# RWKV stage of a two-layer hybrid block: one inverse for both chunks of a step, and the step's preparation written per direction

## The chip, the cores and the metric

One core of one Trainium2 chip runs the whole kernel. The metric is device time in microseconds of one execution; lower is better.

## The reference, cut to what matters

Two layers run over 1024 latent tokens and 256 context tokens with a model width of 1024. Each layer has three branches (gated linear attention, grouped-query attention, RWKV7) and a merge that gates the three. The change is in the RWKV branch, which runs a recurrence forwards and backwards over the tokens, for 8 heads of 64 columns:

```
def step(s, inp):
    r_t, w_t, k_t, v_t, kk_t, a_t = inp
    sa = jnp.einsum('bhvk,bhk->bhv', s, kk_t)
    s = (s * w_t[:, :, None, :] - sa[..., None] * (kk_t * a_t)[:, :, None, :]
         + v_t[..., None] * k_t[:, :, None, :])
    return s, jnp.einsum('bhvk,bhk->bhv', s, r_t)
...
g1, g2, g3 = _split(mg, MERGE_COLS)
m = (jax.nn.sigmoid(g1) * (ya @ w_o_gla) + jax.nn.sigmoid(g2) * (yb @ w_o_att)
     + jax.nn.sigmoid(g3) * (yc @ w_o_rwkv))
```

The kernel does not walk token by token. It takes chunks of 64 tokens, in which the recurrence becomes a set of small matrix products and the inverse of a triangular 64x64 matrix per head and direction.

## The kernel before, in words

The 1280 tokens are 10 tiles of 128. A **step** handles one tile for the forward direction (d = 0) and one for the backward direction (d = 1); it holds two **chunks** of 64 tokens, so a layer has 20 chunks, `q = 2 * step + c`. The RWKV stage of a layer is `rwkv()`, a generator that interleaves five kinds of work, each itself a generator that yields after its matmuls:

- `elem(step)` (L870 to L931), once per step, loads `lt`, `k`, `kk` and `r` for both directions. For each direction it makes the up-projection on TensorE (`ps_t<-lt,wup`), then tanh on ScalarE, a scan, and products on VectorE and GpSimd. They end in `AR` (L910, L912) and `BK` (L920, L924), the two operands of the chunk's products, and `PC`.
- `gram(q)` (L934 to L988), once per chunk, multiplies `BK` with `AR` for each direction (`ps_t<-AR,BK`, 16 instructions), copies one part to `Ms` on ScalarE (L955) and the masked rest to `G` on VectorE (L956), and transposes `BK` into `BKT`. Then it inverts the 16x16 blocks on the diagonal: `Ms` is stored to `nscr` in DRAM (L960), the blocks are loaded as `Lm`, 64 partitions of one 16x16 block each (L962), 15 pairs of VectorE instructions (`mt`, L974, and `acc`, L977) build the inverse in `acc`, which is stored to `tscr` (L978) and, transposed by ScalarE, to `dscr` (L981). `DT` (L983) and `Dg` (L986) load them back in the layout that TensorE wants. `UV` (L945) loads the values.
- `merge(q)` (L991 to L1025) joins the block inverses to the 64x64 inverse `T`. Its first matmuls are `ps_u<-DT,G`; three more rounds follow, each with a copy or an addition into `T` on VectorE (L1021, L1023).
- `chain(q)` (L1027 to L1117) is the recurrence: it uses `T`, `G`, `BKT`, `UV` and the state `S`, and gives `X` (L1050), `UV` (L1061, L1063), the new `S`, and the outputs.
- `finish` (L1119 to L1149) normalises a tile whose two directions are both done.

`spread` runs a set of such generators as threads. Each has a start and an end as shares of the set's time, and the thread that is furthest behind goes next. For each chunk `rwkv()` (L1151 to L1176) makes a set: the chain of `q`, the merge of `q + 1`, `gram(q + 2)` and, for even `q`, `elem` of the next step. So an inverse of chunk `q + 2` starts one whole chain and merge ahead of its own merge.

`weave` (L201) mixes this main thread with fill, the matmuls of `merge_gates` (L1182 to L1210: `ps_mm` and `ps_o` with `wh` and `wl`, 128x512): after each yield of the main thread as much fill is issued as its weight times the ratio allows, and a fill instruction may not be issued before the eighth last yield of the main thread. A scheduler then orders the instructions of each engine; an engine executes its own list in order. The DMAs are issued by SyncE, in order too: one that waits holds up all behind it.

The pools hold three buffers of `G`, `BKT` and `UV`, two of `BK`, four of `AR`, and one each of `Ms`, `Lm`, `acc`, `DT` and `Dg`.

Of the kernel before, what the change touches and what calls it, by code (L numbers as in the profile page):

```python
# [9 lines left out]
F32 = mybir.dt.float32  # L10
F32R = mybir.dt.float32r
AF = mybir.ActivationFunctionType
ALU = mybir.AluOpType
# [16 lines left out]
def consts():  # L30
# [35 lines left out]
    c["ident16"] = np.tile(np.eye(16, dtype=np.float32).reshape(1, 256), (64, 1))  # L66
# [4 lines left out]
def hybrid_kernel(ctx: ExitStack, tc: tile.TileContext, I: dict, C: dict, out: bass.AP):  # L71
# [102 lines left out]
    NSCR = 3  # L174
    nscr, dscr, tscr = [[dt(f"{x}scr{i}", [64, 1040]) for i in range(NSCR)] for x in "ndt"]

# [3 lines left out]
    def full(z):  # L180
        return z.rearrange("(u i) x -> u (i x)", i=4)[:, 0:4096].rearrange("u (s t) -> s u t", t=64)
# [120 lines left out]
    zero = zp.tile([64, 1040], F32, name="zero")  # L302
# [30 lines left out]
    for l in range(DEPTH):  # L333
# [493 lines left out]
        gmask, id16 = rload("gmask", [128, 128]), rload("ident16", [64, 256])  # L827
# [35 lines left out]
        def elem(step):  # L863

            live = need_ctx or step >= 2
            o = {"AR": [], "BK": [], "PC": rp.tile([128, 2, 8], F32, tag="PC", bufs=3, name=nm("PC"))}
            ld = {}
            lt = re_.tile([128, 2, 128], F32, tag="lt", bufs=1, name=nm("lt"))
            for d in range(2):
                c = slice(128 * blk_of(step, d), 128 * blk_of(step, d) + 128)  # L870
                for j in range(2):
                    dma(out=lt[64 * j:64 * j + 64, d], in_=lora[64 * d:64 * d + 64, j, c])
                for x in ("kk", "k", "r"):
                    if x == "r" and not live:
                        continue
                    ld[x, d] = re_.tile([128, 4, 128], F32, tag="ld_" + x, bufs=2, name=nm("ld_" + x))
                    dma(out=ld[x, d], in_=rscr[x][:, c].rearrange("(m p) n -> p m n", p=128))
            for d in range(2):
                t0 = 128 * blk_of(step, d)

                def tk(x):
                    v = ld[x, d]
                    if d:
                        v = v[:, :, ::-1]
                    return v.rearrange("p m (c i) -> p m c i", c=2)

                sc, av = tmp(), tmp()
                pz = [ps("t"), ps("t")]
                for p in range(4):
                    for j in range(2):  # L890
                        hr = slice(64 * j, 64 * j + 64)
                        x = lt[hr, d, :]
                        pe.matmul(pz[j][:, 128 * p:128 * p + 128], wup[d][hr, 128 * p:128 * p + 128], x[:, ::-1] if d else x, start=True, stop=True)
                yield 1.8
                for j, dst, bi, s in ((0, sc, 0, 0.5), (1, av, 2, -0.5)):
                    for p in range(4):
                        act(out=dst[:, p, :], in_=pz[j][:, 128 * p:128 * p + 128], func=AF.Tanh, scale=0.5, bias=prm[:, bi + d, p:p + 1])
                    pool.tensor_scalar(out=dst, in0=dst, scalar1=s, scalar2=s, op0=ALU.mult, op1=ALU.add)
                L = tmp()
                vec.tensor_tensor_scan(out=L.rearrange("p m i -> p (m i)"), data0=smask, data1=sc.rearrange("p m i -> p (m i)"), initial=0.0, op0=ALU.mult, op1=ALU.add)  # L900
                Pt = rp.tile([128, 8, 65], F32, tag="Pt", bufs=1, name=nm("Pt"))
                vec.memset(Pt[:, :, 0:1], 1.0)
                L8 = L.rearrange("p m (c i) -> p (m c) i", c=2)
                act(out=Pt[:, :, 1:65], in_=L8, func=AF.Exp, scale=-DECAY)
                act(out=L8, in_=L8, func=AF.Exp, scale=DECAY)
                vec.tensor_copy(out=o["PC"][:, d, :].unsqueeze(2), in_=Pt[:, :, 64:65])
                Pi = L.rearrange("p m (c i) -> p m c i", c=2)
                AR = rp.tile([128, 4, 2, 2, 64], F32, tag="AR", bufs=4, name=nm("AR"))
                Pv = Pt.rearrange("p (m c) i -> p m c i", c=2)
                vec.tensor_tensor(out=AR[:, :, :, 0, :], in0=Pv[:, :, :, 0:64], in1=tk("kk"), op=ALU.mult)  # L910
                if live:
                    vec.tensor_tensor(out=AR[:, :, :, 1, :], in0=Pv[:, :, :, 1:65], in1=tk("r"), op=ALU.mult)  # L912
                else:
                    vec.memset(AR[:, :, :, 1, :], 0.0)
                BK = rq.tile([128, 4, 2, 2, 64], F32, tag="BK", bufs=2, name=nm("BK"))
                av4 = av.rearrange("p m (c i) -> p m c i", c=2)
                ka = tmp()
                ka4 = ka.rearrange("p m (c i) -> p m c i", c=2)
                pool.tensor_tensor(out=ka4, in0=tk("kk"), in1=av4, op=ALU.mult)  # L919
                vec.tensor_tensor(out=BK[:, :, :, 0, :], in0=ka4, in1=Pi, op=ALU.mult)  # L920
                for p in range(4):
                    pool.tensor_scalar(out=av[:, p, :], in0=av[:, p, :], scalar1=prm[:, 6, p:p + 1], scalar2=prm[:, 7, p:p + 1], op0=ALU.mult, op1=ALU.add)  # L922
                vec.tensor_tensor(out=av4, in0=av4, in1=tk("k"), op=ALU.mult)
                vec.tensor_tensor(out=BK[:, :, :, 1, :], in0=av4, in1=Pi, op=ALU.mult)  # L924
                o["AR"].append(AR)
                o["BK"].append(BK)
                if live:

                    pool.tensor_tensor(out=ka, in0=av[:, :, ::-1] if d else av, in1=ld["r", d], op=ALU.mult)
                    dma(out=wscr[d][:, t0:t0 + 128].rearrange("(m p) n -> p m n", p=128), in_=ka)  # L930
            return o  # L931

        def gram(q, es, step):

            c, e = q % 2, es[step]
            o = dict(e)
            G = rq.tile([128, 2, 2, 4, 128], F32, tag="G", bufs=3, name=nm("G"))
            BKT = rq.tile([128, 2, 4, 128], F32, tag="BKT", bufs=3, name=nm("BKT"))
            UV = rq.tile([128, 2, 4, 2, 64], F32, tag="UV", bufs=3, name=nm("UV"))
            Ms = rq.tile([64, 2, 2, 4, 64], F32, tag="Ms", bufs=1, name=nm("Ms"))  # L940
            o["G"], o["BKT"], o["UV"] = G, BKT, UV
            for d in range(2):
                t0 = 128 * blk_of(step, d)
                v = vtm[d, t0 + 64 * c:t0 + 64 * c + 64, :]
                dma(out=UV[64:128, d].rearrange("p m h i -> p (m h i)"), in_=v)  # L945
            for d in range(2):
                AR, BK = e["AR"][d], e["BK"][d]
                pg = [ps("t"), ps("t")]
                for p in range(4):
                    for h in range(2):  # L950
                        r = slice(64 * h, 64 * h + 64)
                        pe.matmul(pg[h][:, 128 * p:128 * p + 128], BK[r, p, c].rearrange("p a i -> p (a i)"), AR[r, p, c].rearrange("p a i -> p (a i)"), start=True, stop=True)
                yield 2.0
                for h in range(2):
                    act(out=Ms[:, h, d], in_=pg[h][0:64].rearrange("p (u i) -> p u i", u=4)[:, :, 0:64], func=AF.Copy)  # L955
                    vec.tensor_tensor(  # L956
                        out=G[:, h, d], in0=pg[h].rearrange("p (u i) -> p u i", u=4),
                        in1=gmask.unsqueeze(1).to_broadcast([128, 4, 128]), op=ALU.mult)
            ns, ds, ts = nscr[q % NSCR], dscr[q % NSCR], tscr[q % NSCR]
            dma(out=full(ns), in_=Ms.rearrange("p h d m t -> p (h d m) t"))  # L960
            Lm = rq.tile([64, 16, 16], F32, tag="Lm", bufs=1, name=nm("Lm"))
            dma(out=Lm, in_=diag(ns))  # L962
            acc = rq.tile([64, 16, 16], F32, tag="acc", bufs=1, name=nm("acc"))
            vec.tensor_copy(out=acc.rearrange("p a b -> p (a b)"), in_=id16)
            mt = rq.tile([64, 16, 16], F32, tag="mt", bufs=1, name=nm("mt"))
            for d in range(2):
                pt = ps("t")
                for p in range(4):
                    pe.transpose(pt[:, 128 * p:128 * p + 128], e["BK"][d][:, p, c].rearrange("p a i -> p (a i)"), ident)
                yield 0.5  # L970
                act(out=BKT[:, d].rearrange("p m i -> p (m i)"), in_=pt, func=AF.Copy)
# [179 lines left out]
        def rwkv():  # L1151
# [3 lines left out]
            def put(d, key, steps):  # L1155
                d[key] = yield from steps
# [214 lines left out]
```

## Time and profile before

| what | value |
|---|---|
| median of 3 runs | 4006.45 us (4003.45 to 4014.16) |
| the profiled execution | 3994.97 us |
| its span | 3993.2 us |
| TensorE busy | 3737.1 us, 94% |
| weight loads of TensorE busy | 3135.2 us, 79% |
| VectorE busy | 2101.7 us, 53% |
| ScalarE busy | 1649.8 us, 41% |
| GpSimd busy | 934.1 us, 23% |
| mean granted clock of TensorE | 0.958 |
| the RWKV stages in the span | 1022 to 1856 us and 3030 to 3760 us |

PE is TensorE's matmuls, PEld its weight loads, DVE VectorE, ACT ScalarE, POOL GpSimd, SP SyncE. Busy shares are means over all stages. The granted clock is a share of full speed (2.4 GHz). A wait is an engine's idle time, put down to the work whose end released it. Names such as `ps_t<-AR,BK` are output and inputs of an instruction by the names of the program. A line that reads L85 is that of the helper through which all matmuls go, so matmuls are told apart by their tiles.

### The profile page before, as it was taken

How to read it: one execution, taken by the hardware profiler on the slowest of the kernel's cores; microseconds unless marked ns; L12 is line 12 of the kernel's file. 1: busy time of each engine (PE TensorE's matmuls, PEld its weight loads, DVE VectorE, ACT ScalarE, POOL GpSimd, SP SyncE). 2: the span in 40 equal slices, each digit the busy share in tenths (PEclk: the TensorE clock that was granted, in tenths of full speed). 3: DMA queues.
4: the chain of work that ended last, by engine and by line, in shares of the span. 5: the costliest groups of instructions: out<-in, count | busy, mean ns of one | idle time of the engine just before them, and what ended most of it. 6: DMA issues, size and time to landing. Idle time of an engine off the chain costs nothing.

```text
span 3993.2 us, 82346 instructions
## 1 busy us (share of the span) xinstructions
PE 3737.1 (94%) x32356; PEld 3135.2 (79%) x32356; DVE 2101.7 (53%) x4932; ACT 1649.8 (41%) x4135; POOL 934.1 (23%) x1072
## 2 busy tenths in 40 slices
PE   5999999999889898899998999999998898988999
PEld 3699888888777787677877898888886776766787
DVE  3234445456576676654453244455565766665462
ACT  3244435456434444434133344354474334344322
POOL 2133220000232322310333042300002323223042
PEclk7999999999989999999999999999998899889999
DMA  7723225312365667556544132253124556655553
GB/s 228 247 59 89 55 79 169 103 54 84 99 146 124 143 157 187 146 135 193 159 139 132 52 96 70 76 159 116 48 70 108 117 128 143 152 136 134 178 157 113
DMA packets 826613, 497.24 MB, mean 125 GB/s; under 512 B 303152, under 2 KB 760176, under 8 KB 824176
## 3 DMA queue, kind: packets, MB, share of 16 engines
q1 hardware_dynamic: 826224, 491.97, 45.0%
q8 instruction: 254, 4.16, 0.5%
q14 instruction: 135, 1.11, 0.1%
HBM read 340.02 MB, written 151.81 MB: 123 GB/s over the span
## 4 chain that ended last, share of the span: by engine, by line
PE 68%; DMA 11%; DVE 8%; POOL 4%; issue 4%; ACT 3%; SPq 2%; POOLq 0%; DVEq 0%; ACTq 0%
PE ps_mm L85 27%; PE ps_a L85 17%; PE ps_o L85 12%; PE ps_u L85 6%; PE ps_t L90 3%; PE ps_t L85 2%; DMA nscr<-Ms 2%; DMA Lm<-nscr 2%; POOL tmp L922 1%; DVE mt L974 1%; DVE acc L977 1%; DMA wr<-in_w_in_dram 1%; DVE wl L343 1%; DMA tscr<-acc 1%; POOL tmp L919 1%
## 5 line engine op out<-in xcount | busy, mean ns | idle before, releaser
L85 PE MATMUL ps_mm<-h,wh 128*128 128x512 f32 (+1 forms) x2496 | 764.5, 389 | 10.1 <-ACT wh L342 7.7
L85 PEld LDWEIGHTS ps_mm<-h,wh 128*128 128x128 f32 x2496 | 452.5, 196 | 105.2 <-issue 11.7
L343 DVE TENSOR_TENSOR wl<-wr,wh 128x512 fp32r<-128x512 f32 (+1 forms) x464 | 334.5, 743 | 296.7 <-ACT wh L342 292.5
L85 PE MATMUL ps_mm<-h,wl 128*128 128x512 f32 (+1 forms) x1248 | 473.8, 380 | 1.7 <-DVE wl L343 1.7
L342 ACT ACTIVATE wh<-wr 128x512 fp32r<-128x512 f32 (+1 forms) x464 | 271.5, 622 | 420.1 <-PE ps_mm L85 161.4
L85 PE MATMUL ps_mm<-wh,h 128*128 128x256 f32 x2032 | 400.4, 290 | 9.5 <-ACT wh L342 5.9
L85 PEld LDWEIGHTS ps_mm<-wh,h 128*128 128x128 f32 x2032 | 327.7, 194 | 26.0 <-issue 10.7
L85 PE MATMUL ps_a<-h,wh 128*128 128x512 f32 (+1 forms) x1024 | 300.1, 369 | 0.0
L85 PE MATMUL ps_mm<-wl,h 128*128 128x256 f32 x1016 | 293.4, 289 | 0.4 <-DVE wl L343 0.2
L85 PE MATMUL ps_o<-h,wh 128*128 128x512 f32 (+1 forms) x928 | 287.7, 392 | 0.6 <-DVE M L1265 0.6
L85 PEld LDWEIGHTS ps_mm<-h,wl 128*128 128x128 f32 x1248 | 243.6, 195 | 47.8 <-issue 4.0
L974 DVE TENSOR_TENSOR mt<-Lm,acc 64x15 f32<-64x15 f32 (+2 forms) x600 | 129.4, 216 | 163.7 <-DMA Lm<-nscr 146.0
L803 POOL TENSOR_TENSOR y<-y,sg 128x128 f32<-128x128 f32 x64 | 30.2, 472 | 755.1 <-DVE nb L794 369.0
L85 PEld LDWEIGHTS ps_a<-h,wh 128*128 128x128 f32 x1024 | 183.7, 189 | 28.3
L85 PEld LDWEIGHTS ps_mm<-wl,h 128*128 128x128 f32 x1016 | 196.7, 194 | 7.4 <-issue 4.9
L85 PE MATMUL ps_o<-wh,h 128*128 128x256 f32 x976 | 196.7, 289 | 3.5 <-ACT h L286 3.2
L85 PEld LDWEIGHTS ps_o<-h,wh 128*128 128x128 f32 x928 | 167.9, 197 | 34.2 <-issue 2.2
L85 PE MATMUL ps_a<-h,wl 128*128 128x512 f32 (+1 forms) x512 | 188.6, 368 | 0.0
L776 DVE TENSOR_REDUCE mx<-ps_mm 128x1 f32<-128x512 f32 (+1 forms) x200 | 117.9, 594 | 111.1 <-PE ps_mm L85 108.0
L85 PE MATMUL ps_o<-h,wl 128*128 128x512 f32 (+1 forms) x464 | 176.1, 380 | 0.0
L85 PEld LDWEIGHTS ps_o<-wh,h 128*128 128x128 f32 x976 | 158.5, 193 | 10.7 <-issue 5.3
L1006 POOL COPY T<-Dg 128x512 f32<-128x512 f32 x40 | 30.0, 749 | 566.2 <-DMA Dg<-dscr 527.2
(326 smaller groups left out, 8125.2 us busy)
## 6 DMA issues: line engine op xcount, KB each, us to landing
wr<-in_w_in_dram SPq DMA_DIRECT2D x376, 256.0 KB, 3.5
tg<-th SPq DMA_DIRECT2D x96, 256.0 KB, 3.4
th<-tg SPq DMA_DIRECT2D x96, 256.0 KB, 2.9
wm<-in_w_mod_dram SPq DMA_DIRECT2D x16, 1024.0 KB, 7.1
ld_k<-rscr_k SPq DMA_DIRECT2D x40, 256.0 KB, 3.6
ld_kk<-rscr_kk SPq DMA_DIRECT2D x40, 256.0 KB, 3.7
UV<-vtm SPq DMA_DIRECT2D x80, 128.0 KB, 3.2
nscr<-Ms SPq DMA_DIRECT2D x40, 256.0 KB, 3.8
```

The source lines that it names most:

```text
L85: PE.last = nc.tensor.matmul(*a, **k)
L90: PE.last = nc.tensor.transpose(*a, **k)
L342: act(out=hi, in_=src, func=AF.Copy)
L343: vec.tensor_tensor(out=lo, in0=src, in1=hi.bitcast(F32), op=ALU.subtract)
L776: vec.tensor_reduce(out=mx[:, i:i + 1], in_=s[:, :n], axis=AX.X, op=ALU.max, negate=True)
L803: pool.tensor_tensor(out=y[:, hc], in0=y[:, hc], in1=sg[:, hc], op=ALU.mult)
L919: pool.tensor_tensor(out=ka4, in0=tk("kk"), in1=av4, op=ALU.mult)
L922: pool.tensor_scalar(out=av[:, p, :], in0=av[:, p, :], scalar1=prm[:, 6, p:p + 1], scalar2=prm[:, 7, p:p + 1], op0=ALU.mult, op1=ALU.add)
L974: vec.tensor_tensor(out=mt[:, :n, :w], in0=Lm[:, j, j + 1:16].unsqueeze(2).to_broadcast([64, n, w]), in1=acc[:, j:j + 1, :w].to_broadcast( ...
L977: vec.tensor_tensor(out=acc[:, j + 1:16, :w], in0=acc[:, j + 1:16, :w], in1=mt[:, :n, :w], op=ALU.add)
L1006: pool.tensor_copy(out=T.rearrange("p d m t -> p (d m t)"), in_=Dg.rearrange("p d m t -> p (d m t)"))
```

## The change

The diff replaces `gram(q)` and its place in the schedule.

- `prep(os, step)` prepares both chunks of a step: elementwise work of direction 0, products of both chunks for direction 0, elementwise work of direction 1, products of both chunks for direction 1, then one `inverse(step)`. Each chunk's `Ms` goes to its half of a scratch of 128 rows.
- `inverse` loads one `Lm` with 128 partitions (64 blocks of either chunk), runs the 15 pairs of products once, and stores `tscr` and `dscr` once. `DT` and `Dg` are loaded per chunk.
- `elem` has a direction as its argument; `lt` has two buffers of one direction each.
- `G` and `BKT` have four buffers, `Dg` two; `DT` shares two buffers with `Ms`; `acc`, `mt` and `Lm` have 128 partitions; there are two scratches in place of three.
- `UV` is loaded in `merge`.
- `rwkv()` makes a set of threads per step: both chains in turn, the merge of the second chunk (0 to 0.35), `prep` of the next step (0 to 0.6), and the merge of the next step's first chunk (0.75 to 1).
- `dynamic_dma_scratch_size=1024` is given when the program is made. All DMAs of the kernel are on SyncE's queue.

The core of the diff:

```diff
+        def prep(os, step):
+            e = {}
+            yield from elem(step, 0, e)
+            o = [chunk(step, c, e) for c in range(2)]
+            Ms = [None, None]
+            for c in range(2):
+                Ms[c] = rq.tile([64, 2, 2, 4, 64], F32, tag="Ms", bufs=2, name=nm("Ms"))
+                yield from gram(o[c], c, 0, Ms[c])
+            yield from elem(step, 1, e)
+            for c in range(2):
+                yield from gram(o[c], c, 1, Ms[c])
+                dma(out=full(nscr[step % NSCR], c), in_=Ms[c].rearrange("p h d m t -> p (h d m) t"))
+            yield from inverse(step, o)
+            os[2 * step], os[2 * step + 1] = o
...
+        def inverse(step, o):
+            ns, ds, ts = nscr[step % NSCR], dscr[step % NSCR], tscr[step % NSCR]
+            Lm = rq.tile([128, 16, 16], F32, tag="Lm", bufs=1, name=nm("Lm"))
             dma(out=Lm, in_=diag(ns))
+            acc = rq.tile([128, 16, 16], F32, tag="acc", bufs=1, name=nm("acc"))
...
             for j in range(15):
                 n, w = 15 - j, j + 1
                 vec.tensor_tensor(
+                    out=mt[:, :n, :w], in0=Lm[:, j, j + 1:16].unsqueeze(2).to_broadcast([128, n, w]),
+                    in1=acc[:, j:j + 1, :w].to_broadcast([128, n, w]), op=ALU.mult)
                 vec.tensor_tensor(out=acc[:, j + 1:16, :w], in0=acc[:, j + 1:16, :w], in1=mt[:, :n, :w], op=ALU.add)
+                if j % 5 == 4:
+                    yield 0.0
             dma(out=diag(ts), in_=acc)
...
+            for c in range(2):
+                DT = o[c]["DT"] = rq.tile([64, 2, 2, 4, 64], F32, tag="Ms", bufs=2, name=nm("DT"))
+                dma(out=DT.rearrange("p h d m t -> p (h d m) t"), in_=full(ts, c))
...
+            for w in spread([(prep(os, 0), 0.0, 0.7, whole_prep), (merge(os, 0), 0.8, 1.0, whole_merge)]):
                 yield 2.5 * w
-            for q in range(nq):
-                ths = [(chain(q, os.pop(q)), 0.0, 1.0, 8.3 + 6 * 2.0 + 12 * 2.0 if q % 2 else 8.3 + 6 * 2.0)]
-                if q + 1 < nq:
-                    ths.append((merge(os, q + 1), *((0.4, 0.9), (0.65, 1.0))[q % 2], 3.3 + 4 * 2.0))
-                if q + 2 < nq:
-                    ths.append((put(os, q + 2, gram(q + 2, es, (q + 2) // 2)), *((0.55, 0.9), (0.1, 0.5))[q % 2], 5.0 + 6 * 2.0))
-                if q % 2 == 0 and q // 2 + 1 < NTILE and q:
-                    ths.append((put(es, q // 2 + 1, elem(q // 2 + 1)), *(0.0, 0.45), 3.6 + 4 * 2.0))
+            for step in range(NTILE):
+                ths = [(both(step), 0.0, 1.0, whole_chain), (merge(os, 2 * step + 1), 0.0, 0.35, whole_merge)]
+                if step + 1 < NTILE:
+                    ths.append((prep(os, step + 1), 0.0, 0.6, whole_prep))
+                    ths.append((merge(os, 2 * step + 2), 0.75, 1.0, whole_merge))
                 yield from spread(ths)
```

How the order of the instructions changes shows at two places, both around the merge of a step's first chunk in the second layer. On TensorE before, chunk 2's merge (`ps_u<-DT,G`) stands behind the end of the preceding merge and the chain's product with `X` and `T`; `ps_mm` is fill, `ps_t<-lt,wup` the up-projection of the next step:

```order
L90 MATMUL ps_t_33704<-c_ident,BK_33095 128x128 x4
L90 MATMUL ps_t_33716<-c_ident,BK_33157 128x128 x4
L85 MATMUL ps_u_33493<-T_33348,ET_32612 16x16 x16
L85 MATMUL ps_t_33903<-lt_33884,wup_32272 128x128 x4
L85 MATMUL ps_t_33904<-lt_33884,wup_32272 128x128 x4
L85 MATMUL ps_a_33620<-X_33552,T_33348 64x64 x5
L85 MATMUL ps_a_33621<-X_33552,T_33348 64x64 x5
...
L85 MATMUL ps_u_33763<-DT_33545,G_33392 64x48 x16
```

Its inverse was made from products that stand ahead of the whole chain of the chunk before.

On TensorE with the change the same merge stands behind the up-projection and the first products of the step after it (`AR_33484`, `BK_33487`), with three fill matmuls in between:

```order
L85 MATMUL ps_mm_33227<-h_22963,wh_33217 128x512 x2
L85 MATMUL ps_mm_33227<-h_22963,wl_33218 128x512
L85 MATMUL ps_t_33427<-lt_33416,wup_31887 128x128 x4
L85 MATMUL ps_t_33428<-lt_33416,wup_31887 128x128 x4
L85 MATMUL ps_t_33504<-AR_33484,BK_33487 128x128
L85 MATMUL ps_t_33505<-AR_33484,BK_33487 128x128
...
L85 MATMUL ps_mm_33689<-h_22956,wh_33679 128x512 x2
L85 MATMUL ps_mm_33689<-h_22956,wl_33680 128x512
L85 MATMUL ps_u_33287<-DT_33272,G_32848 64x48 x16
```

So the merge has moved from behind a whole chain to right behind the next step's first products. On VectorE with the change, the middle of the 15 pairs of that inverse (`mt_33237`, `acc_33235`) holds the elementwise work of the next step (`AR_33484`, `BK_33487`, which the products above need):

```order
L987 TENSOR_TENSOR acc_33235<-acc_33235,mt_33237 128x11x5
L933 TENSOR_TENSOR AR_33484<-Pt_33479,ld_kk_33419 128x8x64
L935 TENSOR_TENSOR AR_33484<-Pt_33479,ld_r_33423 128x8x64
L984 TENSOR_TENSOR mt_33237<-Lm_33233,acc_33235 128x10x6
L943 TENSOR_TENSOR BK_33487<-tmp_33488,tmp_33477 128x8x64
L925 MEMSET Pt_33773 128x8
L987 TENSOR_TENSOR acc_33235<-acc_33235,mt_33237 128x10x6
L984 TENSOR_TENSOR mt_33237<-Lm_33233,acc_33235 128x9x7
L946 TENSOR_TENSOR tmp_33426<-tmp_33426,ld_k_33421 128x512
L987 TENSOR_TENSOR acc_33235<-acc_33235,mt_33237 128x9x7
L947 TENSOR_TENSOR BK_33487<-tmp_33426,tmp_33477 128x8x64
L984 TENSOR_TENSOR mt_33237<-Lm_33233,acc_33235 128x8x8
```

Before, the products of the inverse that this merge needs (`acc_33474`, the last pairs) stand among the chain's and the merge's copies, with no `AR` or `BK` between them:

```order
L974 TENSOR_TENSOR mt_33476<-Lm_33472,acc_33474 64x3x13
L343 TENSOR_TENSOR wl_33870<-wr_33871,wh_33869 128x512
L977 TENSOR_TENSOR acc_33474<-acc_33474,mt_33476 64x3x13
L343 TENSOR_TENSOR wl_33870<-wr_33875,wh_33869 128x512
L974 TENSOR_TENSOR mt_33476<-Lm_33472,acc_33474 64x2x14
L956 TENSOR_TENSOR G_33597<-ps_t_33659,gmask_32268 128x512
L956 TENSOR_TENSOR G_33597<-ps_t_33660,gmask_32268 128x512
L977 TENSOR_TENSOR acc_33474<-acc_33474,mt_33476 64x2x14
L1023 COPY T_33348<-ps_u_33450 32x8x32
L974 TENSOR_TENSOR mt_33476<-Lm_33472,acc_33474 64x15
L977 TENSOR_TENSOR acc_33474<-acc_33474,mt_33476 64x15
```

The pairs of the inverse and the next step's elementwise work share one stretch of VectorE's list now.

## Rows read from the trace of the kernel before

**Rows 1.** The page, busy time, share and instructions of each engine.

```profile
PE 3737.1 (94%) x32356; PEld 3135.2 (79%) x32356; DVE 2101.7 (53%) x4932; ACT 1649.8 (41%) x4135; POOL 934.1 (23%) x1072
```

**Rows 2.** Table by stage: stretch, length, busy (count) per engine, granted clock, DMA share, GB/s.

```profile
1022.00:1856.00 834.00, 748.33 (x9352) 614.32 (x9352) 521.38 (x1255) 342.29 (x770) 227.02 (x242) 0.93 0.61 148
3030.00:3760.00 730.00, 647.54 (x8368) 511.88 (x8368) 463.47 (x1160) 286.29 (x651) 209.79 (x217) 0.90 0.56 133
```

**Rows 3.** Table by stretch, around a wait of 4 us.

```profile
1390.00:1396.00 6.00, 2.70 (x75) 2.46 (x71) 4.97 (x6) 1.82 (x4) 4.16 (x4) 0.96 1.03 215
1396.00:1404.00 8.00, 7.31 (x121) 6.87 (x123) 7.94 (x15) 3.22 (x10) 4.44 (x5) 0.61 1.03 277
```

**Rows 4.** Waits of TensorE: what released it, us in total, times, longest.

```profile
PE ps_u L85 <- DMA DT<-tscr: 22.2, 11, 4.3
PE ps_t L85 <- DVE BK L924: 20.6, 7, 8.0
PE ps_u L85 <- DVE T L1021: 17.2, 10, 4.0
PE ps_a L85 <- DVE X L1050: 11.6, 6, 3.7
```

**Rows 5.** Groups by line on VectorE: count, busy us, mean ns, idle before.

```profile
L977 DVE TENSOR_TENSOR acc<-acc,mt 64x15 f32<-64x15 f32 (+2 forms) x600 | 130.2, 217 | 17.0
L974 DVE TENSOR_TENSOR mt<-Lm,acc 64x15 f32<-64x15 f32 (+2 forms) x600 | 129.4, 216 | 163.7 <-DMA Lm<-nscr 146.0 <-DMA dscr<-accT 2.2
L1061 DVE COPY UV<-ps_a 64x512 f32<-64x512 f32 x40 | 27.0, 676 | 5.1 <-PE ps_a L85 4.7
L1050 DVE TENSOR_TENSOR X<-ps_a,X 128x512 f32<-128x512 f32 x38 | 26.2, 690 | 7.3 <-PE ps_a L85 6.4
```

**Rows 6.** Timeline of TensorE (start, us): last products of a chunk, and its merge.

```profile
1191.23 1.16 PE L85 MATMUL ps_t<-AR,BK 64*128 64x128 f32 x8
...
1223.09 1.14 PE L85 MATMUL ps_u<-DT,G 64*64 64x48 f32 x32
```

**Rows 7.** Timeline of SyncE's queue, the same inverse.

```profile
1196.33 0.60 SPq L962 DMA_DIRECT2D Lm<-nscr  x1
...
1209.48 0.62 SPq L978 DMA_DIRECT2D tscr<-acc  x1
...
1212.16 0.59 SPq L983 DMA_DIRECT2D DT<-tscr  x1
```

**Rows 8.** Timeline of VectorE, first and last of that inverse's 30 products.

```profile
1198.94 0.18 DVE L974 TENSOR_TENSOR mt<-Lm,acc 64x15 f32<-64x15 f32 x1 [1.14 <-DMA Lm<-nscr]
...
1209.29 0.17 DVE L977 TENSOR_TENSOR acc<-acc,mt 64x15 f32<-64x15 f32 x1
```

**Rows 9.** The page, DMA issues: count, KB each, us to landing.

```profile
DT<-tscr SPq DMA_DIRECT2D x40, 256.0 KB, 4.3
Dg<-dscr SPq DMA_DIRECT2D x80, 128.0 KB, 4.2
```

**Rows 10.** Timeline of TensorE: 16 products, then fill matmuls in threes.

```profile
1355.61 1.16 PE L85 MATMUL ps_t<-AR,BK 64*128 64x128 f32 x16
1356.70 0.73 PE L85 MATMUL ps_mm<-h,wh 128*128 128x512 f32 x2
...
1357.51 0.62 PE L85 MATMUL ps_mm<-h,wh 128*128 128x512 f32 x2
```

**Rows 11.** Timeline, end of an up-projection on TensorE and its BK on VectorE.

```profile
1511.18 0.80 PE L85 MATMUL ps_t<-lt,wup 64*128 64x128 f32 x4
...
1522.55 0.69 DVE L924 TENSOR_TENSOR BK<-tmp,tmp 128x512 f32<-128x512 f32 x1
```

**Rows 12.** Timeline of TensorE, the stage's first up-projection and the products behind it.

```profile
1051.28 1.71 PE L85 MATMUL ps_t<-lt,wup 64*128 64x128 f32 x16
...
1061.84 2.08 PE L85 MATMUL ps_t<-AR,BK 64*128 64x128 f32 x16 [7.96 <-DVE BK L924]
```

**Rows 13.** Loads of the tile Lm, us from issue to landing.

```profile
DMA to landing us min/median/max: 2.5/2.9/5.5
```

More of the change, by code (lines that the diff above doesn't have):

```diff
@@ L172, in hybrid_kernel, with full @@
     yscr, wscr = dt("yscr", [512, NT]), [dt(f"wscr{i}", [512, NT]) for i in range(2)]
-    NSCR = 3
-    nscr, dscr, tscr = [[dt(f"{x}scr{i}", [64, 1040]) for i in range(NSCR)] for x in "ndt"]
+    NSCR = 2
+    nscr, dscr, tscr = [[dt(f"{x}scr{i}", [128, 1040]) for i in range(NSCR)] for x in "ndt"]
     def diag(z):
         return z[:, 0:1024].rearrange("p (s t) -> p s t", t=64)[:, :, 0:16]
-    def full(z):
-        return z.rearrange("(u i) x -> u (i x)", i=4)[:, 0:4096].rearrange("u (s t) -> s u t", t=64)
+    def full(z, c):
+        return z[64 * c:64 * c + 64].rearrange("(u i) x -> u (i x)", i=4)[:, 0:4096].rearrange("u (s t) -> s u t", t=64)
     def xrow(l, t):
@@ L878, in elem @@
[L878 to L888, printed above, removed]
-                for p in range(4):
[L890 to L953, printed above, removed]
-                for h in range(2):
[L955 to L961, printed above, removed]
@@ new lines, in elem @@
+            lt = re_.tile([128, 128], F32, tag="lt", bufs=2, name=nm("lt"))
+            c = slice(128 * blk_of(step, d), 128 * blk_of(step, d) + 128)
+            for j in range(2):
+                dma(out=lt[64 * j:64 * j + 64], in_=lora[64 * d:64 * d + 64, j, c])
+            for x in ("kk", "k", "r"):
+                if x == "r" and not live:
+                    continue
+                ld[x, d] = re_.tile([128, 4, 128], F32, tag="ld_" + x, bufs=2, name=nm("ld_" + x))
+                dma(out=ld[x, d], in_=rscr[x][:, c].rearrange("(m p) n -> p m n", p=128))
@@ new lines, in elem, with tk @@
+            t0 = 128 * blk_of(step, d)
+            def tk(x):
+                v = ld[x, d]
+                if d:
+                    v = v[:, :, ::-1]
+                return v.rearrange("p m (c i) -> p m c i", c=2)
+            sc, av = tmp(), tmp()
+            pz = [ps("t"), ps("t")]
+            for p in range(4):
+                for j in range(2):
+                    hr = slice(64 * j, 64 * j + 64)
+                    x = lt[hr, :]
+                    pe.matmul(pz[j][:, 128 * p:128 * p + 128], wup[d][hr, 128 * p:128 * p + 128], x[:, ::-1] if d else x, start=True, stop=True)
@@ new lines, in elem @@
+            ka = tmp()
+            ka4 = ka.rearrange("p m (c i) -> p m c i", c=2)
+            pool.tensor_tensor(out=ka4, in0=tk("kk"), in1=av4, op=ALU.mult)
+            vec.tensor_tensor(out=BK[:, :, :, 0, :], in0=ka4, in1=Pi, op=ALU.mult)
+            for p in range(4):
+                pool.tensor_scalar(out=av[:, p, :], in0=av[:, p, :], scalar1=prm[:, 6, p:p + 1], scalar2=prm[:, 7, p:p + 1], op0=ALU.mult, op1=ALU.add)
+            vec.tensor_tensor(out=av4, in0=av4, in1=tk("k"), op=ALU.mult)
@@ L966, in gram @@
[L966 to L971, printed above, removed]
+            mt = rq.tile([128, 16, 16], F32, tag="mt", bufs=1, name=nm("mt"))
             for j in range(15):
@@ L993, in merge @@
             G, Dg, DT = o["G"], o["D"], o["DT"]
+            UV = o["UV"] = rq.tile([128, 2, 4, 2, 64], F32, tag="UV", bufs=3, name=nm("UV"))
+            for d in range(2):
+                t0 = 128 * blk_of(q // 2, d) + 64 * (q % 2)
+                dma(out=UV[64:128, d].rearrange("p m h i -> p (m h i)"), in_=vtm[d, t0:t0 + 64, :])
             T = o["T"] = rq.tile([128, 2, 4, 64], F32, tag="T", bufs=3, name=nm("T"))
```

105 lines of the change are left out of this document (67 added, 38 removed).

## The prediction

> **What bounds the kernel now.** I read the page first, for the engines' shares; then the table by stage, for the two stretches that the change touches; then the waits of TensorE, for what ends its idle time there; last the timeline, for how long one inverse takes and how long one elementwise part takes. The page says that TensorE is busy for 94% of the span [rows 1]. The table by stage gives the two RWKV stages, 834 and 730 us long [rows 2]. TensorE is idle in them for 85.7 + 82.5 = 168 us. The granted clock is 0.93 and 0.90 there, so that full speed for the whole stage would save at most 0.07 x 834 + 0.10 x 730 = 131 us. The clock comes from gaps: after a wait of 4 us the chip grants the 1.2 GHz level, and the 8 us around it run at a mean of 0.61, which costs 0.39 x 8 = 3.1 us [rows 3]; 131 / 3.1 makes about 42 such falls. So some 299 us of 1564 can be won, and all else is matmuls that the change leaves as they are. The waits of TensorE say what the idle time consists of: 22.2 us for DT, the inverse on its way back from DRAM, 20.6 for BK, 17.2 for T and 11.6 for X, with many small ones besides [rows 4]. VectorE is busy for 985 of 1564 us [rows 2], so it sets the end only where a chain runs through it.
>
> **The change part by part, VectorE.** The products of the inverses take 129.4 + 130.2 us for 1200 instructions [rows 5]. With 128 partitions 600 are left. A copy of 64 partitions takes 676 ns and an addition of 128 partitions with the same 512 elements each takes 690 [rows 5], so a product keeps its length and VectorE loses 130 us of work. What stood behind those products wins: T, X, G and BK come sooner. Of the 168 us of idle time 146 are left when DT's 22 are taken out; waits for ScalarE, for tables and for products of TensorE itself stay. I let half of the 146 go: **-73**. The ends are 0, if what is late there is late for another reason, and -102 (70%).
>
> **DT's old waits.** The 11 waits of 22.2 us [rows 4] were those of chunks whose inverse came late; their places are new now, and the new ones are counted below: **-22**.
>
> **The new boundary.** What the order shows decides. One inverse in the trace: the last matmul of its chunk's products ends at 1192.4 [rows 6], Lm is issued at 1196.33 [rows 7], the 30 products run from 1198.94 to 1209.46 with other work of VectorE among them [rows 8], the store tscr is issued at 1209.48 and the load DT at 1212.16, 2.7 us later [rows 7], and DT lands 4.3 us after that [rows 9]: 24.1 us in all. Nobody waited, since the merge that needs it began at 1223.09, 30.7 us after the product [rows 6]. With two chunks in one inverse the first merge of a pair has less behind which to hide. I laid the durations of the timeline (1.09 us for 16 of the products and about as much for a group of 32 small matmuls, 0.81 for three fill matmuls; start to start [rows 10]) on TensorE's order of both kernels. Before, the even chunks have 19.5 to 32.1 us of work between their last product and their merge. Now they have 7.5 to 24.8.
>
> For eleven of the twenty pairs it is worse than a short cover: VectorE has the elementwise work of the next pair's first direction inside the 30 products, and TensorE has that direction's up-projection (ps_t<-lt,wup) just ahead of the merge. So the inverse cannot end before the next BK. In the trace the up-projection ends at 1511.98 and BK at 1523.24, 11.3 us later [rows 11]. Add 1 us for the products that stand behind BK (one to four pairs in most of the eleven, 0.22 us each [rows 5]), 2.7 for the store [rows 7], 4.3 for the load [rows 9]: DT lands 19.3 us after the up-projection. The work between it and the merge is, for the eleven, 1.1, 4.6, 3.0, 5.7, 1.1, 1.9, 2.0, 4.6, 3.8, 3.8 and 3.8 us, 35.4 in sum. So 11 x 19.3 - 35.4 = **177 us** of new waits, first for BK (the products of the next pair follow the up-projection with 0 to 3.5 us between) and then for DT. Behind the waiting matmul stand the fill, the later rounds of that merge and the chain of the next pair, so nothing fills the gap. The other nine have the plain 24.1 us against covers of 22.2, 18.1, 16.7, 24.8, 20.9, 21.1, 20.9, 20.0 and 18.4: shortfalls of 1.9, 6.0, 7.4, 0, 3.2, 3.0, 3.2, 4.1 and 5.7, **34.5 us**.
>
> Bounds: once in the trace, at the stage's start, the products follow their up-projection at once; TensorE then begins them 8.9 us after its end, 7.96 of them waiting [rows 12]. The shortest landing of such a load is 2.5 us [rows 13]. A boundary could so cost 8.9 + 1 + 2.7 + 2.5 = 15.1, the eleven 11 x 15.1 - 35.4 = 131, and the other nine, with 22.3, 20. Upwards, the larger Lm (twice the rows, 2.9 us now [rows 13]) could take as long as DT, 4.3, which adds 1.4 to each of the nine. I take nothing for it, since Dg with 128 KB lands in 4.2 and DT with 256 KB in 4.3 [rows 9]. The Trainium skill ("DMA: Bandwidth & Descriptors", section "Anatomy of one DMA — SWDGE (gpsimd) path") gives about 2.0 us plus the bytes at 436 GB/s, for a DMA that GpSimd issues. By it the store would take 2.3 and the load 2.6, an estimate of 2.1 us less for each of twenty boundaries, some 40 us less in the sum; the rows, 2.7 and 4.3 on SyncE's queue, are longer, so this trace does not bear it out and the rows stand.
>
> **Clock.** 42 falls go with 168 us of idle time. With 73 us of the old idle time left, 73/168 of them, 18, stay, and 15 of the new waits are longer than the 4 us of rows 3 (the eleven, and four of the nine): 33 in place of 42, **-28 us** at 3.1 each. The ends are -59 (23 left) and 0.
>
> **What costs nothing.** 60 DMAs fewer on SyncE's queue (Lm, tscr and dscr are issued once for two chunks): it waits for nothing that TensorE lacks other than DT. The UV load now stands in the merge, behind DT and Dg on that queue; its user is the chain after the merge, several rounds later. DT takes the buffers of Ms, so the next pair's copies to Ms wait for the merge that reads DT; the merge stands right behind those products in the order, and the transposes that need the bank come after. The prologue's changed weight moves three fill groups.
>
> **Sum.** On the profiled execution of 3994.97: +177 +34.5 -73 -22 -28 = +88.5, 4083.5. The median of the runs shown, 4006.45, stands 11.5 above that execution, so the time is **4095**. Its own range goes from the low ends of the waits with my gains (+131 +20 -123 = +28, 4035) to my waits with half of the -73 and no gain in the clock (+211.5 -36 -22 = +153, 4160).
>
> **The rivals.** *Faster.* VectorE's relief is the larger term. For it speaks that T, X, G and BK account for much of the idle time [rows 4] and that the products are what stands ahead of them; against it, that the new order leaves TensorE nothing between the up-projection and the products. With the low ends (+131 +20) and the high gains (-102 -22 -59) the sum is -32: 3963, median 3974. It decides where the eleven waits fall below a mean of 8.0 us with my gains ((73 + 22 + 28 - 34.5) / 11), or below 14.8 us with the high gains ((183 - 20) / 11); I have 177 / 11 = 16.1. Chance 0.30. *No change.* The waits only change places: TensorE's matmuls are the same, VectorE is not full, and what is lost at eleven boundaries returns in the rest, 4006. The Trainium skill ("Perfetto Trace Analysis", section "Identifying the Most-Contended Engine") says to improve the most contended engine first; the change relieves the engine with 53% [rows 1] and leaves the one with 94% its work. By that rule the time stays near 4006. Chance 0.10. *Much slower.* The half of the old waits does not go, since BK's path rather than the products made them, the clock gains nothing, and the second direction's products (8 to 12 us behind their up-projection in most pairs, against 11.3) wait a further 1 us each, 20 us: +177 +34.5 -22 +20 = +210, 4216 at the median. Chance 0.10.
>
> **How the numbers follow.** My forecast has 0.50. A measurement of this kernel can tell 0.3%, 12 us, from no change. Faster by more: the first rival, 0.30. Within: the second, 0.10. Slower: forecast and third, 0.60. The range runs from 3950, below the first rival, to 4210, just short of the third's value; what is left out is 0.2 at most. Forecasts of both signs hold most of the chance, which is why it is wide; the likeliest case's own is 4035 to 4160.
>
> **What would show it.** Right: TensorE's waits for DT and BK sum to 200 us or more in place of 43, in gaps of 8 to 17 us, one per pair; VectorE has 300 + 300 products with the same mean of 216 ns; waits for T and X are about halved; the stages are longer by some 40 to 45 us each. Wrong: DT and BK together below 100 us, or the elementwise path from the up-projection to BK well under 9 us, or products of 128 partitions that take longer than 64.

## The result and the profile after

The changed kernel takes **4169.47 us** at the median of 4 runs (4168.85 to 4178.87), against 4007.47 before: a ratio of 1.041, 95% interval 1.039 to 1.043. The forecast was 4095, slower by 2.2%; it is slower by 4.1%. The profiled execution has a span of 4167.0 us, 174 more than before.

The table by stage, the changed kernel's two RWKV stages (columns as in [rows 2]):

```profile
1020.00:1928.00 908.00, 761.66 (x9348) 627.77 (x9347) 468.60 (x945) 339.84 (x760) 223.47 (x242) 0.90 0.57 136
3096.00:3940.00 844.00, 672.26 (x8404) 540.22 (x8405) 418.17 (x853) 286.02 (x645) 190.82 (x218) 0.86 0.51 118
```

The stages grew from 1564 to 1752 us. TensorE's idle time in them went from 168 to 146.3 + 171.7 = 318 us, its busy time from 1396 to 1434 (36 more instructions lie inside my second cut, 4 fewer in the first). VectorE has 98 us less work there (985 to 887 [rows 2]).

The waits of TensorE in the changed kernel (columns as in [rows 4]):

```profile
PE ps_u L85 <- DMA DT<-tscr: 128.2, 20, 9.8
PE ps_t L85 <- DVE BK L947: 127.0, 21, 11.2
PE ps_t L85 <- DVE acc L987: 10.1, 1, 10.1
PE ps_t L85 <- ACT accT L992: 9.8, 1, 9.8
PE ps_u L85 <- DVE T L1036: 4.6, 3, 2.3
```

The two single waits of 10 us stand at `ps_t<-AR,BK` too, so DT and BK make 275 us, against 22.2 + 20.6 = 43 [rows 4]. DT is waited for once per step, 20 times. All else fell from 125 to 43 us; T at its first addition, 17.2 us before [rows 4], has 4.6.

The products, groups by line on VectorE in the changed kernel (count, busy us, mean ns, idle before); half as many, with means of 267 and 251 ns in place of 217 and 216 [rows 5]:

```profile
L987 DVE TENSOR_TENSOR acc<-acc,mt 128x15 f32<-128x15 f32 (+2 forms) x300 | 80.2, 267 | 8.0
L984 DVE TENSOR_TENSOR mt<-Lm,acc 128x15 f32<-128x15 f32 (+2 forms) x300 | 75.3, 251 | 69.1 <-DMA Lm<-nscr 61.7
```

TensorE's products of `BK` and `AR`, before and with the change (columns as in [rows 5]):

```profile
L85 PE MATMUL ps_t<-AR,BK 64*128 64x128 f32 x1280 | 128.0, 306 | 35.6 <-DVE BK L924 20.6 <-ACT Pt L904 9.0 <-DVE G L956 5.4
L85 PE MATMUL ps_t<-AR,BK 64*128 64x128 f32 x1280 | 159.4, 323 | 146.9 <-DVE BK L947 127.0 <-DVE acc L987 10.1 <-ACT accT L992 9.8
```

The same 1280 instructions take 31 us more. A group of 16 (one chunk, one direction) that stands in one stretch takes 1.16 us [rows 10], and in the trace its products start in pairs, some 6 ns apart. Eight that stand alone start one by one and take 1.16 us as well, so a group in two halves costs twice as much:

```profile
1122.22 1.16 PE L85 MATMUL ps_t<-AR,BK 64*128 64x128 f32 x8
...
1126.17 1.16 PE L85 MATMUL ps_t<-AR,BK 64*128 64x128 f32 x8
```

Of the 80 groups in the two stages 56 stood in one stretch before and 38 do now; the halves of 8 that stand alone went from 22 to 80. Why the scheduler parts them isn't shown.

One step boundary in the second layer, timeline of TensorE:

```profile
3428.96 1.16 PE L85 MATMUL ps_t<-lt,wup 64*128 64x128 f32 x16
...
3441.43 2.08 PE L85 MATMUL ps_t<-AR,BK 64*128 64x128 f32 x16 [8.45 <-DVE BK L947]
3452.16 1.95 PE L85 MATMUL ps_u<-DT,G 64*64 64x48 f32 x32 [8.65 <-DMA DT<-tscr]
```

The same boundary on VectorE (end of BK, last product) and on SyncE's queue:

```profile
3440.60 0.69 DVE L947 TENSOR_TENSOR BK<-tmp,tmp 128x512 f32<-128x512 f32 x1
...
3442.92 0.17 DVE L987 TENSOR_TENSOR acc<-acc,mt 128x15 f32<-128x15 f32 x1
```

```profile
3443.13 1.22 SPq L990 DMA_DIRECT2D tscr<-acc  x1
3444.44 0.91 SPq L993 DMA_DIRECT2D dscr<-accT  x1
3445.40 1.80 SPq L901 DMA_DIRECT2D ld_r<-rscr_r  x1
3447.30 1.32 SPq L996 DMA_DIRECT2D DT<-tscr  x2
```

The up-projection ends at 3430.12 and BK at 3441.29, 11.2 us later (11.3 in [rows 11]). The last products end 1.8 us behind BK. The load DT is issued 4.2 us after the store (2.7 in [rows 7]) and has landed by 3452.16, 4.9 us after its issue. So 22.0 us lie between the up-projection and DT, where the prediction had 19.3.

The clock around it (table by stretch):

```profile
3428.00:3436.00 8.00, 4.99 (x59) 3.45 (x57) 7.48 (x21) 2.48 (x9) 4.00 (x5) 0.99 0.65 182
3436.00:3444.00 8.00, 2.08 (x16) 1.81 (x16) 6.93 (x20) 1.89 (x3) 3.06 (x4) 0.50 0.31 91
3444.00:3452.00 8.00, 0.00 (x0) 0.00 (x0) 0.29 (x1) 0.00 (x0) 0.00 (x0) 0.50 0.92 140
3452.00:3460.00 8.00, 7.84 (x75) 6.22 (x76) 2.40 (x4) 1.48 (x5) 1.23 (x2) 0.51 0.53 67
3460.00:3468.00 8.00, 8.00 (x145) 6.57 (x143) 2.00 (x4) 2.96 (x7) 0.00 (x0) 1.00 0.37 100
```

The clock falls to the 1.2 GHz level in the first wait, stays there through the products between the two waits, the second wait and 8 us behind it: 24 us, where a single wait of 4 us left some 6 [rows 3]. Cut to 1 us, the table by stage shows 40 stretches of low clock (mean under 0.75) in the two stages before, 255 us in all, and 31 in the changed kernel, 418 us: fewer falls, each 13.5 us instead of 6.4. But most of what was added is waiting: TensorE is busy in 214 of the 255 us and in 217 of the 418. Its busy time at the full level rose from 1182 to 1217 us.

### The profile page after: what moved, and what is told of

It reads as the page before. It is cut to its first block, busy times and chain, and to the rows that moved or that the text cites. A ratio compares the mean times of both kernels' runs of the same rounds, so it can differ in the third digit from the quotient of the medians.

```text
span 4167.0 us, 81524 instructions
## 1 busy us (share of the span) xinstructions
PE 3766.2 (90%) x32356; PEld 3170.0 (76%) x32356; DVE 2003.2 (48%) x4312; ACT 1645.5 (39%) x4115; POOL 914.8 (22%) x1072
## 4 chain that ended last, share of the span: by engine, by line
PE 46%; DMA 4%; DVE 4%; issue 3%; POOL 2%; ACT 1%; SPq 1%; POOLq 0%; DVEq 0%; ACTq 0%
PE ps_mm L85 18%; PE ps_a L85 10%; PE ps_o L85 8%; PE ps_u L85 5%; PE ps_t L85 2%; PE ps_t L90 2%; DMA DT<-tscr 1%; DVE mt L984 1%; DVE acc L987 1%; DMA tscr<-acc 1%; POOL tmp L945 1%; DMA nscr<-Ms 1%; DMA Lm<-nscr 1%; DMA ys<-yTgla 0%; POOL tmp L942 0%
## 5 line engine op out<-in xcount | busy, mean ns | idle before, releaser
L85 PE MATMUL ps_t<-AR,BK 64*128 64x128 f32 x1280 | 159.4, 323 | 146.9 <-DVE BK L947 127.0
L85 PEld LDWEIGHTS ps_t<-AR,BK 64*128 64x128 f32 x1280 | 134.2, 221 | 171.2 <-issue 143.4
L966 DVE TENSOR_TENSOR G<-ps_t,gmask 128x512 f32<-128x512 f32 x160 | 106.2, 687 | 237.9 <-ACT Ms L965 237.7
L921 POOL TENSOR_SCALAR tmp<-tmp 128x512 f32<-128x512 f32 x80 | 53.7, 672 | 708.9 <-ACT tmp L920 696.6
L85 PE MATMUL ps_u<-DT,G 64*64 64x48 f32 x1280 | 61.4, 259 | 128.2 <-DMA DT<-tscr 128.2
```

The costliest lines, as they stand in the source:

```text
L85: PE.last = nc.tensor.matmul(*a, **k)
L966: vec.tensor_tensor(out=o["G"][:, h, d], in0=pg[h].rearrange("p (u i) -> p u i", u=4), in1=gmask.unsqueeze(1).to_broadcast([128, 4, 128]), ...
```

## The experiments

Each has its ratio to the kernel before from its own comparison. "DT and BK" are the waits counted as above, with the few at the same place that the trace puts down to ScalarE's `Pt`; "other" is the rest of TensorE's idle time in the two stages. In these terms: before 52 and 116, the change 275 and 43. Low clock is counted as above.

**Two inverses in the new order.**

```diff
-            yield from inverse(step, o)
+                yield from inverse1(step, c, o)
```

(within the loop over the chunks; `inverse1` is the old inverse on 64 partitions; the buffers, the place of the `UV` load and the scratch size of the change stay)

> The changed kernel with its inverse made per chunk on 64 partitions again (1200 products, a Lm, tscr and dscr each); the order of elementwise work and products, the threads and the buffers stay. Theory (the new order of the work makes the time, through waits for BK behind the up-projection and for DT at the first merge of a step): the time stays near the changed kernel's 4169, between 4110 and 4190; BK's and DT's waits sum to about 200 to 240 us (275 in the changed kernel, 43 before), and waits for T and X come back in part. Rival (the shared inverse makes the time, since the first chunk waits for the second one's products and the wide products are slower): 4000 to 4060, DT's waits near the 22 of before.

4177.91 us, 1.043 (1.041 to 1.045), beside 1.041 for the change: the intervals overlap. DT and BK 171, other 99, granted clock 0.939. The theory's time held, with smaller waits than it said. The shared inverse isn't the loss; undoing it gains nothing in this order. TensorE's idle time in the stages fell from 318 to 270 us, but its busy time rose from 1434 to 1490: the waits are more and shorter, 47 falls of the clock, and matmuls run at the low level for 336 us instead of 217.

**Elementwise work of both directions first.**

```diff
             yield from elem(step, 0, e)
+            yield from elem(step, 1, e)
...
-            yield from elem(step, 1, e)
```

> The changed kernel with the elementwise work of both directions ahead of the products of both; all else as in the change. Theory (the order): the up-projection now has more work between it and its products, BK's waits fall from 137 to about 60 us, DT's stay near 110 to 130, the falls of the clock become fewer, and the time falls to 4030 to 4080. Rival 1 (the shared inverse): above 4140, since the inverse is unchanged. Rival 2 (waits change places, each us saved at BK is waited for DT): above 4140 with DT's waits at 200 or more.

4111.32 us, 1.027 (1.025 to 1.028). BK's waits by name fell from 127 to 43, DT's rose from 128 to 138. Between theory and rivals: about 58 us come from the placement of the elementwise work alone, less than expected, and DT took some of it back.

**Earlier preparation.**

```diff
-                    ths.append((prep(os, step + 1), 0.0, 0.6, whole_prep))
-                    ths.append((merge(os, 2 * step + 2), 0.75, 1.0, whole_merge))
+                    ths.append((prep(os, step + 1), 0.0, 0.42, whole_prep))
+                    ths.append((merge(os, 2 * step + 2), 0.82, 1.0, whole_merge))
```

> The changed kernel with two numbers of its thread table changed: the preparation of the next step ends at 0.42 of the set instead of 0.6, and the merge of its first chunk starts at 0.82 instead of 0.75. Theory (the order's covers): the covers hardly grow, since what stands ahead of the merge is still the next step's up-projection and products; 4120 to 4160, BK's waits near 130 and DT's near 105. Rival (the inverse's cover alone is too short, and any shift of the merge cures it): DT's waits under 50 and 4060 or less.

4155.09 us, 1.037 (1.035 to 1.038): the time as the theory had it. DT 112, BK by name 104, less than it said.

**Both: elementwise work first, later merges** (edit of the second experiment, and windows 0 to 0.38, 0.1 to 0.45, 0.9 to 1).

> Elementwise work of both directions first, and a later merge: preparation 0 to 0.38 of the set, merge of the second chunk 0.1 to 0.45, merge of the next first chunk 0.9 to 1. Theory (the order alone makes the loss, and the shared inverse's relief of VectorE, which took the other waits from 125 to 43 us, is a gain): BK's and DT's waits fall to about 100 us, the granted clock returns to 0.92 or more, and the time is 3950 to 4000, below the kernel before. Rival (the relief of VectorE is worth nothing by itself; the other waits fell only because TensorE waited elsewhere): the other waits rise again to 100 or more and the time is 4020 to 4070.

4068.7 us, 1.015 (1.014 to 1.017). A miss: DT and BK came down to 135 only, other 71, mean clock of the run 0.953. The rival's time, though not its cause. Two edits of order, with the shared inverse untouched, take back 100 of the 162 us. Against the kernel before, TensorE has 37 us more idle time in the stages and 39 more busy time; the products of `BK` and `AR` take 175 us in place of 128.

**Chunks apart in that order** (the last one with `inverse1`).

> The experiment with both directions' elementwise work first and later merges, with the inverse made per chunk on 64 partitions again. Theory (what is left to that experiment's 4069 is the late DT of the shared inverse, one chunk's earlier inverse cures part of it): DT's waits fall from 85 to 40 to 60 us and the time to 4020 to 4050. Rival (what is left is the set of threads per step; VectorE's relief makes up for DT): 4065 to 4100.

4073.67 us, 1.017 (1.015 to 1.018). DT fell to 15, but other rose to 127, the idle time fell only from 205 to 185, and the busy time rose by 31 (360 us of low clock in place of 328). The rival held: what is left is not DT's lateness alone. Part of it is again the products of `BK` and `AR`, 180 us.

**Fill freed and prologue doubled in that order.**

```diff
-                yield 2.5 * w
+                yield 5.0 * w
...
-            weave(rwkv(), merge_gates(), (0.6, 0.53)[l], (0, 8), None)
+            weave(rwkv(), merge_gates(), (0.6, 0.53)[l], (0, 24), None)
```

> The kernel of the experiment with both directions' elementwise work first and later merges, and two numbers of the fill: a fill instruction may be issued up to 24 yields of the main thread early (8 before), and the prologue of a layer draws twice the fill (weight 5 instead of 2.5). Theory (TensorE waits where no fill was left that it may take; the shared inverse itself is a gain): BK's and DT's waits fall from 126 us to 50 to 80, the other waits stay at 60 to 80, the clock in the stages is that of the kernel before or better, and the time is 3940 to 4000, faster than before. Rival (what fill the gaps take is missing later, so that the idle time moves to the end of the stages): 4040 to 4080.

4083.91 us, 1.020 (1.017 to 1.022): nearest the rival, 4 us above its range. BK's waits fell to 12, DT 72, other 117, with more low clock (380 us in place of 328) and 190 us for the products of `BK` and `AR`. Freeing the fill in this way takes nothing back.

**The prologue's weight in the kernel before** (first half of that edit).

> The kernel before with the prologue's weight alone changed from 2.5 to 5, as a control of that number. Theory (waits at the start of a stage are filled): about 20 to 30 us of waits and clock go, 3970 to 3995. Rival (fill taken early is missing late): 4000 to 4020.

3990.16 us, 0.997 (0.996 to 0.999): the theory's time. DT and BK 21, other 134, idle 155 in place of 168.

**The shared inverse alone, in the old order and threads.**

```diff
+            pair[c] = o
+            if c:
+                yield from inverse(step, [pair[0], pair[1]])
```

> The kernel before with the shared inverse alone: elementwise work for both directions, products per chunk and all threads as before, but the 16x16 blocks of both chunks are inverted together on 128 partitions after the second chunk's products (the identity is loaded by a DMA, for want of room). Theory (the new order makes the loss; the shared inverse costs cover at a step's first merge and gains VectorE time): BK's and DT's waits 100 to 140 us (43 before), the other waits fall from 125 to 60 to 90, 4010 to 4070. Rival (the shared inverse is the loss): 4110 or more.

4024.49 us, 1.006 (1.004 to 1.009), inside the theory's range. DT and BK 140, other 80. Its waits for DT, by the waits of TensorE:

```profile
PE ps_u L85 <- DMA DT<-tscr: 89.3, 19, 17.2
PE ps_t L85 <- DVE BK L924: 36.0, 8, 8.8
```

With the first experiment this closes the square: neither 1, shared inverse alone 1.006, new order alone 1.043, both 1.041. The new order is the loss. It shows in the products of `BK` and `AR` too: they take 159 to 190 us in all seven kernels with the new order, and 125 to 136 in all seven with the old one.

**Half the products in the kernel before.**

```diff
-            for j in range(15):
+            for j in range(0, 15, 2):
```

> The kernel before with 8 of the 15 pairs of products of each inverse left out of the count (only every second pair is made, so the inverse isn't complete): what VectorE's relief is worth by itself, without the shared inverse and without the new order. Theory (half of the old idle time stood behind the products): waits other than BK's and DT's fall from 125 to 60 to 80 us and the time to 3930 to 3980. Rival (VectorE is off the path; its relief is worth nothing): 3995 to 4015.

The loop makes 8 of the 15 pairs and leaves out 7. 3990.78 us, 0.997 (0.996 to 0.998), between the two forecasts and near the rival's. VectorE's busy time in the stages fell by 103 us, about as much as with the change, and TensorE's idle time stayed at 169 (DT and BK 30, other 139). VectorE's relief, with the shorter inverse that comes with it here, is worth some 13 us.

**The shared inverse in the old order, with cover.** To the kernel with the shared inverse alone: the windows and the fill limit below, elementwise work from 0 to 0.3 of its set, and prologue weight 5.

```diff
-                    ths.append((merge(os, q + 1), *((0.4, 0.9), (0.65, 1.0))[q % 2], 3.3 + 4 * 2.0))
+                    ths.append((merge(os, q + 1), *((0.4, 0.9), (0.8, 1.0))[q % 2], 3.3 + 4 * 2.0))
...
-                    ths.append((put(os, q + 2, gram(q + 2, es, (q + 2) // 2)), *((0.55, 0.9), (0.1, 0.5))[q % 2], 5.0 + 6 * 2.0))
+                    ths.append((put(os, q + 2, gram(q + 2, es, (q + 2) // 2)), *((0.5, 0.8), (0.0, 0.3))[q % 2], 5.0 + 6 * 2.0))
...
-            weave(rwkv(), merge_gates(), (0.6, 0.53)[l], (0, 8), None)
+            weave(rwkv(), merge_gates(), (0.6, 0.53)[l], (0, 12), None)
```

> The kernel before with the shared inverse alone, and the thread table moved for it: products of the second chunk 0 to 0.3 of their set (0.1 to 0.5 before), of the first 0.5 to 0.8, elementwise work 0 to 0.3, merge of a first chunk from 0.8 (0.65), prologue weight 5, and fill up to 12 yields early. Theory (with cover for its first merge the shared inverse is a gain, and TensorE's long waits at the step boundary are all that spoils it): BK's and DT's waits fall from 140 to 70 to 90 us, 3960 to 3995, below the kernel before. Rival (what cover the merge gets is taken from other waits, as in the run with the free fill, whose other waits rose to 117): 4005 to 4030.

**3956.09 us, 0.987 (0.986 to 0.988)**, faster than both kernels. Its stages and its waits:

```profile
1019.00:1849.00 830.00, 760.41 (x9455) 634.68 (x9455) 483.25 (x960) 348.99 (x777) 232.11 (x242) 0.93 0.65 156
2997.00:3704.00 707.00, 634.49 (x8336) 511.18 (x8335) 403.26 (x830) 272.45 (x626) 199.23 (x211) 0.91 0.59 133
```

```profile
PE ps_u L85 <- DMA DT<-tscr: 47.3, 15, 11.6
PE ps_t L85 <- DVE BK L924: 9.4, 6, 2.4
```

DT and BK 57, other 85, VectorE as light as in the change (887 us), the low clock at 245 us. The time is 4 us below the theory's range.

**Its controls in the kernel before: prologue and fill alone, then also the thread windows.**

> The kernel before with prologue weight 5 and fill up to 12 yields early, without a shared inverse: the control for the run with the shared inverse and the moved threads. By the covers BK's and DT's waits stay at about 20 us (21 with the weight alone): 3980 to 3995. Rival (fill taken early is missing at the end of the stage): 4000 to 4015.

4015.18 us, 1.001 (1.000 to 1.002): the rival; with the fill limit of 12 the prologue's gain is gone.

> The fastest version so far (3956) without its shared inverse: the kernel before with the same thread windows, prologue weight and fill limit, and an inverse per chunk on 64 partitions. Theory (the shared inverse is what gains, once its cover is there): 3985 to 4015, with BK's and DT's waits at 20 to 40 us and the other waits at 120 or more. Rival (the moved threads and the prologue gain by themselves, the shared inverse adds nothing): 3945 to 3970.

3990.05 us, 0.996 (0.995 to 0.997): DT and BK 22, other 125. The windows with prologue and fill are worth 0.4%; the shared inverse takes a further 0.9%, against a loss of 0.6% without its cover. Only 5 us of that gain are idle time of TensorE in the stages (142 in place of 147: 35 us more for DT and BK, 40 less for the rest); 16 are busy time, with 200 us at the low level in place of 218. Why that is so wasn't tested.

## Why the prediction was right, and where its sizes were off

**The boundary was right.** Eleven steps of the trace have the prediction's covers, in its order. They have 102 us of waits at the products and 94 at the merge, 196 us in place of 177, a mean of 17.8 against 16.1. At the boundary shown the elementwise path took 11.2 us for 11.3, the products behind BK 1.8 for 1, the store 4.2 for 2.7 and the load 4.9 for 4.3. The term taken at nothing, the larger Lm, was small: it lands in 3.1 us at the median, against 2.9 [rows 13]. What grew is DT's load, 5.2 us at the median against 4.3 [rows 9]. By the Trainium skill's formula for DMAs that GpSimd issues ("DMA: Bandwidth & Descriptors", section "Anatomy of one DMA — SWDGE (gpsimd) path") it would be 2.6, an estimate; no load of DT in these runs landed in less than 3.7.

The other nine waits for DT sum to 34.3 us for 34.5. That is luck in part: singly they go from 0.9 to 8.8 where the prediction had 0 to 7.4, and one of them stands at a twelfth boundary of the long kind, with 6.6 us for BK ahead of it.

**BK elsewhere.** -73 let BK's old 20.6 us shrink with the rest. Outside the eleven, the waits at the products came to 45 us: 28 at the first steps of the two layers, 6.6 at the twelfth boundary, and 10 in small ones. The third rival had priced 20 more, at the second directions.

**-73 for VectorE's relief: the size came, the reason is half shown.** The other waits fell by 82 us (by 73 in the count of the experiments). But relief without a shared inverse leaves them standing (half the products: 139 for 116), and the new order without relief lowers them too (99). In the four pairs of kernels that differ in the inverse alone, the shared one has fewer other waits each time (80 for 116, 43 for 99, 71 for 127, 85 for 125) and longer ones for DT and BK (by 88, 104, 77 and 35). How the 82 divide between relief and work that caught up while TensorE stood at the boundary is open.

**The clock, and a term that wasn't there, are the steps that failed.** The prediction had 33 falls in place of 42 at 3.1 us each, -28 us. The count was good, 31 for 40. The gain did not come, since the stretches grew: matmuls ran at the low level for 217 us, 214 before. At half speed that costs 107 and 108 us, an estimate from these two numbers; the 131 us of the prediction counted the low clock of waits as well, where it costs nothing. Instead of -28, TensorE's busy time rose by 38, and 36 of these are at the full level, so they aren't the clock's (a few come from the 32 more instructions inside the cuts). The prediction took all else to be matmuls that the change leaves as they are. The products of `BK` and `AR`, more often issued in halves now, take 31 us more, and those of X and T 14 (69.7 for 55.4); over the whole run, where the busy time rose by 29, the others take 17 less. In the stages: +232 (DT and BK) -82 (other) +38 = +188, against a sum of +88.5; the rest of the span lost 14, some of it by where the stages are cut.

The Trainium skill ("TensorE: Matmul & The Clock Gate", section "HAM oscillation — how this bites in real kernels") describes short bursts of matmuls between waits, each of which starts at the low clock again. The trace agrees at the boundary shown, where the products between the two waits and the 8 us behind the second run at the low level.

**The prediction's own signs.** DT and BK came to 275 us, above the 200 it asked for, though in two gaps a step. The products on 128 partitions have longer means, 267 and 251 ns for 217 and 216, which it had named as a sign of being wrong; their medians, 216 and 210 for 201, are near. The stages grew by 74 and 114 us, not by 40 to 45.

**The rivals.** *Faster* asked for cheap boundaries and worth in VectorE's relief. The boundaries were not cheap in this order; in the fastest experiment they were, and the kernel was faster. *No change* fell. *Much slower* had the clock right, which gained nothing, and the old waits wrong.

**What the prediction didn't separate** was the order from the shared inverse. Its boundary term joins both; the square of four kernels gives the order +3.4% to +4.3% and the shared inverse between -0.2% and +0.6%.

## What to carry to other kernels

A batch that shares a long chain delays its first consumer, which has to move back with it; with that cover the same batch that cost 0.6% gained 0.9%. Work out the distance from producer to consumer on the engine that bounds, instruction by instruction, before trusting the relief of another engine. Price the clock by the matmuls that run at the low level, not by the falls or by their length: 418 us at that level held no more work than 255 had. And look whether a new order still issues small matmuls together: here half a group of 16 cost as much as the whole.

## What the runs showed of the hardware that was not expected

Two waits of 8.5 us with 2.1 us of matmuls between them keep TensorE at the 1.2 GHz level for about 24 us on end, of which it is busy for 10.

Sixteen products on 64 rows (the halves of a tile of 128 partitions) take 1.16 us in one stretch, and eight that stand alone take the same 1.16 us.

DT's load of 256 KB, two issued together and four loads of Dg behind them, lands at a median of 5.1 to 5.2 us in the kernels with the shared inverse, 4.1 to 4.3 in those without it. The loads of the changed kernel:

```profile
DMA to landing us min/median/max: 4.0/5.2/6.8
```

Products on 128 partitions have a mean of 267 and 251 ns in the changed kernel, and 224 and 233 in the fastest experiment, against 217 and 216 on 64 partitions [rows 5]. The medians are nearer: 216 and 210 ns in the changed kernel, 209 and 210 in the fastest experiment, 201 and 201 before. The rest of the longer means are single products of 0.3 to 1.3 us, 3% of all before and 10% in the changed kernel; without them the means are 198 and 207 ns. On 128 partitions in the old order (the fastest experiment) 4% are so long, and on 64 in the new order (the first experiment) 7%, so it is the order more than the partitions that makes them; which neighbour does was not tested.
